# Order within a step of attention: the probabilities' split, transposes and read-back against the dense piece, in a two-layer decoder on one core

## The chip, the cores and the metric

The kernel runs on one core of a Trainium2 chip. A core has a matrix engine (TensorE, PE in the profile; its weight loads are PEld), a vector engine (VectorE, DVE), a scalar engine (ScalarE, ACT), a third elementwise engine (GpSimd, POOL) and SyncE (SP), which only issues DMAs here. Each engine runs its own list of instructions strictly in the order in which it was written; semaphores hold an instruction back until what it reads is there or what it overwrites is free. The metric is the device time of one execution in microseconds (us). Times inside an execution come from one profiled execution and count from its first instruction.

## The reference

A two-layer decoder trunk on 512 tokens of width 1024, batch 1. Layer 1 is chunkwise retention, layer 2 is native sparse attention. The change lies in layer 2. What matters of it, cut:

```python
s_c = q @ k_cmp * scale                      # 31 compressed blocks, masked, softmax -> p_c
imp = selection_importance(p_c.sum(heads))   # top 16 of at most 8 blocks of 64: all are selected
p_s = softmax(where(valid_s, q @ k_sel * scale, NEG))     # causal over 512 keys
p_w = softmax(where(valid_w, q @ k_win * scale, NEG))     # window of 512 keys: causal too
o = g0 * (p_c @ v_cmp) + g1 * (p_s @ v_sel) + g2 * (p_w @ v_win)
y = (silu(gate) * o) @ w_out
```

There are 4 groups of 4 heads; keys and values are shared in a group. With 512 tokens both big branches are plain causal attention with their own keys and values, so each head has two of them. Every product is computed in a split form: each operand is a high part plus a low part, and three matmuls (high-high, high-low, low-high) make one.

## The kernel before, in words

**Passes.** The attention loop has 32 passes, written (g, u): group g = 0..3, u = 0..7. Pass u stands for head u // 2 and branch u % 2 of group g. A pass is software-pipelined: it computes scores and exponentials of the *next* pass (`scores`), scales them (`scale_probs`), splits its *own* transposed probabilities into high and low part (`probs_split`), transposes the next pass's probabilities (`probs_T`), and at its end multiplies its own with the values (`values`). Between these stands dense work, the "fillers": projections of the next group's queries, of the gate, and of the output, cut into units of 12 matmuls. `steps` says how many units go to the three places `fill(0)`, `fill(1)`, `fill(2)` of a pass.

**Names and lines of before.** DVE: L949 and L946 add the causal mask to the scores, L953 takes the row maximum, L962 and L963 make the scale factors, L986 makes the low part `tL`, L975 (four of them) transposes 32x32 blocks of the next probabilities into `pt1`, L205 makes the low part of a weight piece, L757 and L744 finish a gate or query projection, L1021 adds a tile of the output projection to the residual, L900 to L903 finish the compressed branch, L916 splits its transposed probabilities, L999 and L1001 gate the head's output `o`. ACT: L954 takes the exponential and its row sum, L985 makes the high part `tH`, L190 the high part of a weight piece, L756 and L743 begin the evacuation of a projection. POOL: L966 (four) scales the probabilities, L176 multiplies a weight piece by its gain, L904 scales the compressed probabilities. SP: L979 (four DMAs) writes `pt1` to a tile `moved` in DRAM, L982 reads it back permuted into `pt2`, L143 loads a weight piece.

**The transposition.** A full 512-wide transposition is made of 32x32 transposes on DVE, four writes to DRAM and one read-back in another order. The read-back waits for the four writes, and the split (L985, L986) waits for the read-back. SP works in order, so whatever stands behind the read-back waits with it.

**Weights.** `Stream` holds the list of weight pieces. `tick(n)` does n times: low part of the oldest piece (DVE) and the next load (SP), high part of the next (ACT), gain of the next but one (POOL). Four raw buffers and six split buffers stand between.

**Banks.** A projection or an output tile needs a PSUM bank of tag `d`, of which there are two, used in turn; PE may write a bank again only after the DVE instruction that empties it.

**Three kinds of passes** come up below. *Gate-and-tile* passes, (0,4), (1,0), (1,4), (2,0), (2,4), (3,0): two units of a gate projection in `fill(0)` and `fill(1)`, then two output tiles in `fill(2)`. *Tile* passes, (0,5), (1,1), (1,5), (2,1), (2,5), (3,1), (3,5): six output tiles, two in each place. *Projection* passes: (0,0) to (0,3), (1,2), (1,3), (2,2), (2,3) and (3,2), (3,3), with gate and query units only; and the last two passes of a group, (g,6) and (g,7), which also hold the next group's key projections and are followed by its value projections.

Of the kernel before, what the change touches and what calls it, by code (L numbers as in the profile page):

```python
# [11 lines left out]
F32 = mybir.dt.float32  # L12
# [21 lines left out]
def between(g, h):  # L34

    def out(g, pair):
        return [("nout", g, 2 * pair), ("nout", g, 2 * pair + 1)]

    if g == 3:
        return ([("gate", 3, 0)] + out(2, 1), [("gate", 3, 1), ("gate", 3, 2)], out(3, 0),  # L40
                [("gate", 3, 3), ("emb", 1, 0), ("emb", 1, 1)])[h]
    q = [("q", g + 1, h - 1), ("q", g + 1, h)]
    if g == 0 and h < 2:
        return q if h else [("gate", 0, 0), ("gate", 0, 1)]
    return [("gate", g, h)] + (q if h % 2 else out(g - (h == 0), int(h == 0)))
# [191 lines left out]
def decoder(ctx: ExitStack, tc: tile.TileContext, x, xT, stream, cst, msk, gains, fnorm, out):  # L237
    nc = tc.nc
# [3 lines left out]
    dr = ctx.enter_context(tc.tile_pool(name="dr", bufs=2, space=bass.MemoryType.DRAM))  # L242
# [7 lines left out]
    def V(o, n):  # L250
        assert o + n <= nF, (o, n)
        return arenaF[:, o:o + n]
# [20 lines left out]
    def psum(tag, shape=None):  # L273
        n = {"d": 2, "s": 3, "pt": 2, "o": 1}[tag]
        return ps.tile([128, 512], F32, name=tag, bufs=n)
# [26 lines left out]
    W = Stream(nc, stream, raw, wh, wl, gain)  # L302
# [172 lines left out]
    def run(g):  # L475
        for _ in g:
            pass
# [219 lines left out]
    pt1, pt2 = V(fb + 2176, 1280), V(fb + 3456, 1280)  # L697
# [33 lines left out]
    def v_pieces(g):  # L731
        if g == 0:
            return [W.get("kvb", r, min(384, 1024 - r), 0, 304) for r in (0, 384, 768)]
        return [W.get("kvv", 512 * a, 512, 256 * g, 256) for a in (0, 1)]
# [27 lines left out]
    def k_proj(g, b):  # L762
        p = W.get("kv", 0, 1024, 1024 + 512 * b + 128 * g, 128)
        o = psum("d")
        wst(p, o)
        if b == 0:
            m = slice(32 * g, 32 * g + 32)
            pool.tensor_copy(k2H[0][:, :32], kcH[:, m].bitcast(F32))
            pool.tensor_copy(k2L[0][:, :32], kcL[:, m].bitcast(F32))
        e = 0 if b else 32  # L770
        split_psum(k2H[b][:, e:], k2L[b][:, e:], o)
        W.tick()
        p.done()
# [134 lines left out]
    def cmp_T(h):  # L908

        p = psum("pt")  # L910
        for i in range(NT):
            pe.transpose(p[:96, 128 * i:128 * i + 128], pc4[h % 2][:, i].rearrange("p r n -> p (r n)"),
                         ident)
        d = pcat[h % 2]
        act.activation(d[:96], p[:96], AF.Copy)
        dve.tensor_sub(d[64:96], p[64:96], d[64:96].bitcast(F32))  # L916

    def scores(g, u):
        h, b = divmod(u, 2)
        e = 0 if b else 32  # L920
        mx, sm_ = scal(4), scal(4)
        cmp = []

        def block(w, i, lo, hi):
            c = slice(128 * i, 128 * i + 128)
            mm3(w, [(q2H[h][:, c], q2L[h][:, c], k2H[b][:, lo:hi], k2L[b][:, lo:hi])], True, True)

        for bank in ((3,), (2,), (0, 1)):
            o = psum("s")
            f, at = 0, []  # L930
            for i in bank:
                lo = e if i == 3 else 0
                n = 128 * i + 128 + e - lo
                block(o[:, f:f + n], i, lo, lo + n)
                at.append(f + e - lo)
                f += n
            if e and 2 in bank:
                block(o[:, 416:448], 3, 0, 32)
                cmp.append((2, o[:, 0:448].rearrange("p (a n) -> p a n", a=14)[:, 0:14:13]))
            elif e and 0 in bank:  # L940
                cmp.append((0, o[:, 0:480].rearrange("p (a n) -> p a n", a=3)[:, 0:2, :32]))
            if 1 in bank:

                d = bass.AP(tensor=o.tensor, offset=o.offset + e,
                            ap=[list(o.ap[0]), [256 + e, 2], [1, 128]])
                dve.tensor_add(d, d, tri[:, None, :].to_broadcast([128, 2, 128]))  # L946
            else:
                d = o[:, at[0] + 128 * bank[0]:][:, :128]
                dve.tensor_add(d, d, tri)  # L949
            for i, f in zip(bank, at):  # L950
                n = 128 * i + 128
                w = o[:, f:f + n]
                dve.reduce_max(mx[:, i:i + 1], w, axis=mybir.AxisListType.X, negate=True)  # L953
                act.activation(P[:, PO[i]:PO[i] + n], w, AF.Exp, bias=mx[:, i:i + 1],  # L954
                               accum_out=sm_[:, i:i + 1])
        chain = cmp_probs(g, h, cmp) if e else iter(())
        next(chain, 0)
        return sm_, chain

    def scale_probs(g, u, sm_):  # L960
        h, b = divmod(u, 2)
        dve.reciprocal(sm_, sm_)  # L962
        dve.tensor_mul(sm_, sm_, bg[:, :, 12 * g + 3 * h + b + 1])  # L963
        for i in (3, 2, 0, 1):
            w = P[:, PO[i]:PO[i] + 128 * i + 128]
            pool.tensor_scalar(w, w, sm_[:, i:i + 1], 1.0, op0=OP.mult, op1=OP.mult)  # L966

    def view(a, o, *ap):
        return bass.AP(tensor=a.tensor, offset=a.offset + o, ap=[list(a.ap[0])] + [list(d) for d in ap])

    def probs_T():


        for j in range(NT):
            dve.transpose(view(pt1, JB[j], (32, NT - j), (320, 4), (1, 32)),  # L975
                          view(P, PO[j] + 128 * j, (384, NT - j), (32, 4), (1, 32)))
        m = dr.tile([128, 1280], F32, name="moved")
        for a in range(4):
            nc.sync.dma_start(bass.AP(tensor=m.tensor, offset=m.offset + 320 * a,  # L979
                                      ap=[[1280, 32], [32 * 1280, 4], [1, 320]]),  # L980
                              pt1[32 * a:32 * a + 32].rearrange("p (b n) -> p b n", b=4))
        nc.sync.dma_start(pt2, m)  # L982

    def probs_split():
        act.activation(tH, pt2, AF.Copy)  # L985
        dve.tensor_sub(tL, pt2, tH.bitcast(F32))  # L986
# [36 lines left out]
    def fillers(g):  # L1023
        for kind, *i in (b for h in range(4) for b in between(g, h)):
            yield from {"gate": g_proj, "q": q_proj, "nout": pair_tiles, "emb": emb_tiles}[kind](*i)
# [4 lines left out]
    sums, chain = scores(0, 0)  # L1030
    scale_probs(0, 0, sums)
    next(comp1)
    w2p.done()
    probs_T()
    run(chain)
    k_proj(0, 1)

# [3 lines left out]
    for g in range(GROUPS):  # L1041
        f = fillers(g)
        for u in range(8):
            h = u // 2
            last = (g, u) == (3, 7)
            W.auto = False
            left = 2 * len(between(g, h))
            first = 4 if h == 3 else left // 2
            n = PLAN[u] if g == 3 else left - first if u % 2 else first
            steps = [1, 1, 0] if last else PARTS[n]  # L1050

            def fill(i):
                for _ in range(steps[i]):
                    next(f)

            sums = None
            if u < 7:
                nxt = g, u + 1
            elif g < 3:
                k_proj(g + 1, 0)  # L1060
                k_proj(g + 1, 1)
                nxt = g + 1, 0
            else:
                nxt = None
            if nxt:
                sums, chain = scores(*nxt)
            fill(0)
            if sums is not None:
                scale_probs(*nxt, sums)
            next(chain, 0)  # L1070
            fill(1)
            probs_split()
            if sums is not None:
                probs_T()
            W.tick(0 if last else 2)
            next(chain, 0)
            if u % 2 == 0:
                cmp_T(h)
            fill(2)
            if u % 2 == 0:  # L1080
                o_head = psum("o")
            values(g, u, o_head)
            W.auto = True
        run(f)
        if g < 3:
            p = v_pieces(g + 1)
            for t in range(NT):
                v_proj(g + 1, t, p, ("d", "pt")[t % 2], t % 2)
# [101 lines left out]
```

## Time and profile before

| | |
|---|---|
| time, median of 3 runs | 1251.55 us (1251.02 to 1253.88) |
| the profiled execution's own time | 1248.97 us |
| its span, first to last instruction | 1247.2 us |
| PE busy | 1146.7 us, 92% of the span |
| DVE busy | 753.4 us, 60% |
| ACT busy | 485.5 us, 39% |
| POOL busy | 324.9 us, 26% |
| mean granted clock of PE | 0.960 |

The profiled execution is 1.8 us longer than its span and 2.6 us under the median of the runs. Busy shares are means over the whole program: layer 1 and layer 2's projections fill the first 590 us, the attention loop goes from 590 to about 1174 us. In the rows below the first number is a start in us, the second a duration, and square brackets give how long the engine had stood idle before and what ended that.

### The profile page before, as it was taken

To read this page: it belongs to the slowest core of one execution; us is meant where nothing else is said; L and a number is where in the kernel's file an instruction comes from. 1 tells how busy PE (TensorE), PEld (TensorE's weight loads), DVE (VectorE), ACT (ScalarE), POOL (GpSimd) and SP (SyncE) were. 2 spreads that over 40 slices of the span, in tenths; PEclk is the share of its full clock that TensorE was granted. 3 is DMA by queue.
4 is the path that set the end of the run, shared out by engine and by line. 5 is a ranking of instruction groups with operands and counts; after the bars stand their busy time and mean duration, and the time that the engine had idled before them with its cause. 6 is when DMAs were issued, how large, how long until landed. Compare 5 with 4: busy or idle time off the path is not lost. (4 is left out here: it accounts for less than half of the span.)

```text
span 1247.2 us, 14924 instructions
## 1 busy us (share of the span) xinstructions
PE 1146.7 (92%) x5486; PEld 961.9 (77%) x5486; DVE 753.4 (60%) x1290; ACT 485.5 (39%) x852; POOL 324.9 (26%) x357
## 2 busy tenths in 40 slices
PE   9999999999999999997878898879988799878797
PEld 7888888888888888886767787768877688666686
DVE  4745446346435565566666656776576766777455
ACT  6432233233234554464333334442344323443454
POOL 0121012003002123556242304243134422221102
PEclk9999999999999999999788999999999899979899
DMA  8422322322322313454343333443424443353311
GB/s 326 138 73 85 105 85 85 101 93 68 105 81 68 115 39 124 155 161 135 99 150 119 110 118 115 152 135 106 138 83 146 135 135 110 107 170 124 99 51 68
DMA packets 52633, 143.84 MB, mean 115 GB/s; under 512 B 6096, under 2 KB 22736, under 8 KB 52560
## 3 DMA queue, kind: packets, MB, share of 16 engines
q1 hardware_dynamic: 52128, 142.10, 35.4%
q8 instruction: 43, 0.70, 0.2%
q10 hardware_dynamic: 432, 0.79, 0.2%
q14 instruction: 30, 0.25, 0.1%
HBM read 119.80 MB, written 23.07 MB: 115 GB/s over the span
## 5 line engine op out<-in xcount | busy, mean ns | idle before, releaser
L356 PE MATMUL d<-arenaR 128*128 128x512 f32 (+2 forms) x2904 | 686.2, 391 | 39.7 <-DVE arenaF L1021 27.2
L356 PEld LDWEIGHTS d<-arenaR 128*128 128x128 f32 x2904 | 538.4, 193 | 152.9 <-DVE arenaF L1021 32.3
L356 PE MATMUL s<-arenaR 128*128 128x512 f32 (+8 forms) x1182 | 249.1, 363 | 3.4 <-ACT arenaF L954 1.8
L356 PEld LDWEIGHTS s<-arenaR 128*128 128x128 f32 x1182 | 208.6, 197 | 35.1 <-ACT arenaF L954 2.0
L205 DVE TENSOR_TENSOR arenaR<-arenaF,arenaR 128x1024 fp32r<-128x1024 f32 (+1 forms) x142 | 179.6, 1282 | 67.0 <-ACT arenaR L190 66.8
L190 ACT ACTIVATE arenaR<-arenaF 128x1024 fp32r<-128x1024 f32 (+1 forms) x142 | 145.9, 1046 | 120.4 <-PE s L356 68.4
L356 PE MATMUL o<-arenaR 128*128 128x512 f32 (+3 forms) x744 | 148.5, 351 | 42.3 <-ACT arenaR L985 21.9
L356 PEld LDWEIGHTS o<-arenaR 128*128 128x128 f32 x744 | 126.3, 209 | 65.2 <-ACT arenaR L985 25.9
L176 POOL TENSOR_TENSOR arenaF<-arenaF 128x512 f32<-128x512 f32 x108 | 126.2, 1190 | 154.8 <-DMA arenaF<-stream_dram 150.4
L966 POOL TENSOR_SCALAR arenaF<-arenaF 128x512 f32<-128x512 f32 (+3 forms) x128 | 84.5, 678 | 231.2 <-ACT arenaR L985 79.8
L954 ACT ACTIVATE arenaF<-s,arenaF 128x512 f32<-128x512 f32 (+3 forms) x128 | 67.6, 528 | 134.4 <-DVE arenaF L953 132.3
L372 POOL TENSOR_TENSOR arenaF<-arenaF 128x1 f32<-128x1 f32 (+1 forms) x25 | 14.2, 568 | 292.3 <-DVE arenaF L371 292.3
L953 DVE TENSOR_REDUCE arenaF<-s 128x1 f32<-128x512 f32 (+3 forms) x128 | 62.8, 491 | 22.9 <-ACT arenaF L954 19.6
L356 PE MATMUL pt<-arenaR 128*128 128x512 f32 (+1 forms) x384 | 75.9, 349 | 0.0
L975 DVE STREAM_TRANSPOSE arenaF<-arenaF 128x512 f32<-128x512 f32 (+3 forms) x128 | 57.7, 489 | 25.0 <-POOL arenaF L966 23.9
L356 PEld LDWEIGHTS pt<-arenaR 128*128 128x128 f32 x384 | 62.8, 189 | 9.4
L209 DVE SCALAR_TENSOR_TENSOR arenaR<-arenaF,arenaR 128x512 fp32r<-128x512 f32 x64 | 45.7, 762 | 35.0 <-PE pt L356 21.4
L986 DVE TENSOR_TENSOR arenaR<-arenaF,arenaR 128x1280 fp32r<-128x1280 f32 x32 | 50.4, 1575 | 19.6 <-ACT arenaR L985 19.6
L194 ACT ACTIVATE arenaR<-arenaF 128x512 fp32r<-128x512 f32 x64 | 43.1, 720 | 46.5 <-issue 22.3
L1000 ACT ACTIVATE arenaR<-arenaF 128x512 fp32r<-128x512 f32 x16 | 10.1, 633 | 130.0 <-DVE arenaF L999 130.0
L1021 DVE TENSOR_TENSOR arenaF<-arenaF,d 128x512 f32<-128x512 f32 x64 | 42.0, 682 | 25.1 <-PE d L356 24.8
L985 ACT ACTIVATE arenaR<-arenaF 128x1280 fp32r<-128x1280 f32 x32 | 40.6, 1267 | 2.8 <-DMA arenaF<-moved 2.7
(125 smaller groups left out, 741.5 us busy)
## 6 DMA issues: line engine op xcount, KB each, us to landing
arenaF<-stream_dram SPq DMA_DIRECT2D x174, 512.0 KB, 4.2
moved<-arenaF SPq DMA_DIRECT2D x128, 160.0 KB, 2.8
arenaF<-moved SPq DMA_DIRECT2D x32, 640.0 KB, 4.0
arenaF<-xT_dram SPq DMA_DIRECT2D x8, 256.0 KB, 4.8
arenaF<-x_dram SPq DMA_DIRECT2D x4, 512.0 KB, 7.6
out_dram<-arenaF SPq DMA_DIRECT2D x3, 512.0 KB, 2.7
arenaF<-cst_dram SPq DMA_DIRECT2D x4, 256.0 KB, 3.9
arenaF<-stream_dram ACTq DMA_DIRECT2D x2, 256.0 KB, 3.4
```

Of the source, the lines that this page charges most:

```text
L176: self.nc.gpsimd.tensor_mul(r3[:, k], r3[:, k], g[:, k, None].to_broadcast([128, m // 2, w]))
L190: self.nc.scalar.activation(hi[:, :m * w], raw, AF.Copy)
L194: self.nc.scalar.activation(hi[:, c], raw[:, c], AF.Copy, scale=g[:, k:k + 1])
L205: self.nc.vector.tensor_sub(lo[:, :m * w], raw, hi[:, :m * w])
L209: self.nc.vector.scalar_tensor_tensor(lo[:, c], raw[:, c], g[:, k:k + 1], hi[:, c], op0=OP.mult, op1=OP.subtract)
L356: pe.matmul(o, a, b, start=start and i == 0, stop=stop and i == n - 1)
L953: dve.reduce_max(mx[:, i:i + 1], w, axis=mybir.AxisListType.X, negate=True)
L954: act.activation(P[:, PO[i]:PO[i] + n], w, AF.Exp, bias=mx[:, i:i + 1], accum_out=sm_[:, i:i + 1])
L966: pool.tensor_scalar(w, w, sm_[:, i:i + 1], 1.0, op0=OP.mult, op1=OP.mult)
L975: dve.transpose(view(pt1, JB[j], (32, NT - j), (320, 4), (1, 32)), view(P, PO[j] + 128 * j, (384, NT - j), (32, 4), (1, 32)))
L986: dve.tensor_sub(tL, pt2, tH.bitcast(F32))
L1021: dve.tensor_add(d, d, o)
```

## The change

Within a pass the order becomes: scores of the next pass, `fill(0)`, scaling, split of the own probabilities, exponential of the compressed branch, one tick, transposes and writes, `fill(1)`, the second tick, the rest of the compressed branch, `fill(2)`, read-back, values. Before, `fill(1)` stood ahead of the split, both ticks followed the writes and the read-back followed the writes at once. Nothing is computed otherwise. In the new file the lines are shifted: L975 is L977, L979 is L981, L982 is L986, L985 and L986 are L989 and L990, L999, L1001 and L1021 are L1003, L1005 and L1025. The texts keep the old numbers.

```diff
     def probs_T():
         for j in range(NT):
             dve.transpose(view(pt1, JB[j], (32, NT - j), (320, 4), (1, 32)), ...
-        m = dr.tile([128, 1280], F32, name="moved")
+        m = moved[0] = dr.tile([128, 1280], F32, name="moved")
         for a in range(4):
             nc.sync.dma_start(...)
-        nc.sync.dma_start(pt2, m)
+
+    def probs_back():
+        nc.sync.dma_start(pt2, moved.pop(0))
...
             if sums is not None:
                 scale_probs(*nxt, sums)
+            probs_split()
             next(chain, 0)
-            fill(1)
-            probs_split()
+            W.tick(0 if last else 1)
             if sums is not None:
                 probs_T()
-            W.tick(0 if last else 2)
+            fill(1)
+            W.tick(0 if last else 1)
             next(chain, 0)
             if u % 2 == 0:
                 cmp_T(h)
             fill(2)
+            if sums is not None:
+                probs_back()
```

DVE in the gate-and-tile pass (1,0), from the scale factors to the next pass's scores, before:

```order
L962 RECIPROCAL arenaF<-arenaF 128x4
L963 TENSOR_TENSOR arenaF<-arenaF 128x4
L757 SCALAR_TENSOR_TENSOR arenaF<-arenaF,d 128x512
L986 TENSOR_TENSOR arenaR<-arenaF,arenaR 128x1280
L975 STREAM_TRANSPOSE arenaF<-arenaF 128x4x4x32
L975 STREAM_TRANSPOSE arenaF<-arenaF 128x3x4x32
L975 STREAM_TRANSPOSE arenaF<-arenaF 128x2x4x32
L975 STREAM_TRANSPOSE arenaF<-arenaF 128x4x32
L205 TENSOR_TENSOR arenaR<-arenaF,arenaR 128x1024
L916 TENSOR_TENSOR arenaR<-pt,arenaR 32x512
L1021 TENSOR_TENSOR arenaF<-arenaF,d 128x512 x2
```

and the same stretch now (L990 is the low part, L977 the transposes, L1025 the tiles' adds):

```order
L962 RECIPROCAL arenaF<-arenaF 128x4
L963 TENSOR_TENSOR arenaF<-arenaF 128x4
L990 TENSOR_TENSOR arenaR<-arenaF,arenaR 128x1280
L977 STREAM_TRANSPOSE arenaF<-arenaF 128x4x4x32
L977 STREAM_TRANSPOSE arenaF<-arenaF 128x3x4x32
L977 STREAM_TRANSPOSE arenaF<-arenaF 128x2x4x32
L977 STREAM_TRANSPOSE arenaF<-arenaF 128x4x32
L757 SCALAR_TENSOR_TENSOR arenaF<-arenaF,d 128x512
L205 TENSOR_TENSOR arenaR<-arenaF,arenaR 128x1024
L916 TENSOR_TENSOR arenaR<-pt,arenaR 32x512
L1025 TENSOR_TENSOR arenaF<-arenaF,d 128x512 x2
```

The evacuation of the gate's bank, L757, has moved from ahead of the low part to behind the transposes.

DVE in the tile pass (1,1), from the adds of `fill(0)`'s tiles to the last low part of a weight piece, before:

```order
L1021 TENSOR_TENSOR arenaF<-arenaF,d 128x512 x2
L962 RECIPROCAL arenaF<-arenaF 128x4
L963 TENSOR_TENSOR arenaF<-arenaF 128x4
L1021 TENSOR_TENSOR arenaF<-arenaF,d 128x512 x2
L986 TENSOR_TENSOR arenaR<-arenaF,arenaR 128x1280
L975 STREAM_TRANSPOSE arenaF<-arenaF 128x4x4x32
L975 STREAM_TRANSPOSE arenaF<-arenaF 128x3x4x32
L975 STREAM_TRANSPOSE arenaF<-arenaF 128x2x4x32
L975 STREAM_TRANSPOSE arenaF<-arenaF 128x4x32
L205 TENSOR_TENSOR arenaR<-arenaF,arenaR 128x1024 x2
```

and now:

```order
L1025 TENSOR_TENSOR arenaF<-arenaF,d 128x512 x2
L962 RECIPROCAL arenaF<-arenaF 128x4
L963 TENSOR_TENSOR arenaF<-arenaF 128x4
L990 TENSOR_TENSOR arenaR<-arenaF,arenaR 128x1280
L205 TENSOR_TENSOR arenaR<-arenaF,arenaR 128x1024
L977 STREAM_TRANSPOSE arenaF<-arenaF 128x4x4x32
L977 STREAM_TRANSPOSE arenaF<-arenaF 128x3x4x32
L977 STREAM_TRANSPOSE arenaF<-arenaF 128x2x4x32
L977 STREAM_TRANSPOSE arenaF<-arenaF 128x4x32
L1025 TENSOR_TENSOR arenaF<-arenaF,d 128x512 x2
L205 TENSOR_TENSOR arenaR<-arenaF,arenaR 128x1024
```

The adds of `fill(1)`'s two tiles stand behind the low part, one L205 and the transposes, where they stood ahead of all of them.

SP from the writes of pass (1,1) to those of (1,2), before:

```order
L979 DMA moved<-arenaF 32x4x320 x4
L982 DMA arenaF<-moved 128x1280
L143 DMA arenaF<-stream_dram 128x1024 x2
L979 DMA moved<-arenaF 32x4x320 x4
L982 DMA arenaF<-moved 128x1280
```

and now (L981 the writes, L986 the read-back):

```order
L981 DMA moved<-arenaF 32x4x320 x4
L143 DMA arenaF<-stream_dram 128x1024
L986 DMA arenaF<-moved 128x1280
L143 DMA arenaF<-stream_dram 128x1024
L981 DMA moved<-arenaF 32x4x320 x4
```

Of the two weight loads of a pass one now goes out ahead of the writes and one between the writes and the read-back; before, both stood behind the read-back. POOL's list is the same in both kernels, and so is PE's.

## Rows read from the trace of the kernel before

**Rows 1.** Waits of PE over the whole span: us in total, times, longest

```profile
PE d L356 <- DVE arenaF L1021: 27.2, 16, 3.4
PE o L356 <- ACT arenaR L985: 21.9, 11, 3.0
PE o L356 <- DVE arenaR L986: 13.2, 12, 1.6
PE d L356 <- DVE arenaF L757: 11.9, 4, 4.8
```

**Rows 2.** Timeline, first mask add of a pass, on DVE: start, duration

```profile
606.54 0.29 DVE L949 TENSOR_TENSOR s<-s,masks 128x128 f32<-128x128 f32 x1
...
669.06 0.29 DVE L949 TENSOR_TENSOR s<-s,masks 128x128 f32<-128x128 f32 x1
...
703.25 0.29 DVE L949 TENSOR_TENSOR s<-s,masks 128x128 f32<-128x128 f32 x1
...
753.71 0.29 DVE L949 TENSOR_TENSOR s<-s,masks 128x128 f32<-128x128 f32 x1
...
766.70 0.29 DVE L949 TENSOR_TENSOR s<-s,masks 128x128 f32<-128x128 f32 x1
...
787.05 0.29 DVE L949 TENSOR_TENSOR s<-s,masks 128x128 f32<-128x128 f32 x1
...
821.39 0.29 DVE L949 TENSOR_TENSOR s<-s,masks 128x128 f32<-128x128 f32 x1
```

**Rows 3.** Timeline, the gate-and-tile pass (1,0)

```profile
757.60 0.19 ACT L954 ACTIVATION_READ_ACCUMULATOR arenaF<-s,arenaF 128x1 f32 x1
...
758.17 1.27 ACT L985 ACTIVATE arenaR<-arenaF 128x1280 fp32r<-128x1280 f32 x1
758.31 0.69 DVE L757 SCALAR_TENSOR_TENSOR arenaF<-arenaF,d 128x512 f32<-128x512 f32 x1
758.37 3.29 POOL L966 TENSOR_SCALAR arenaF<-arenaF 128x512 f32<-128x512 f32 x4 [2.69 <-ACT arenaF L756]
...
759.48 1.49 DVE L986 TENSOR_TENSOR arenaR<-arenaF,arenaR 128x1280 fp32r<-128x1280 f32 x1 [0.48 <-ACT arenaR L985]
...
761.69 1.84 DVE L975 STREAM_TRANSPOSE arenaF<-arenaF 128x512 f32<-128x512 f32 x4 [0.73 <-POOL arenaF L966]
```

**Rows 4.** Timeline, the tile pass (1,1)

```profile
772.41 7.36 PE L356 MATMUL d<-arenaR 128*128 128x512 f32 x24 [3.19 <-DVE arenaF L1021]
...
773.42 2.06 POOL L966 TENSOR_SCALAR arenaF<-arenaF 128x512 f32<-128x512 f32 x4 [9.76 <-ACT arenaR L985]
...
780.83 2.32 DVE L205 TENSOR_TENSOR arenaR<-arenaF,arenaR 128x1024 fp32r<-128x1024 f32 x2
...
785.06 0.68 DVE L999 SCALAR_TENSOR_TENSOR arenaF<-o,arenaF 128x512 f32<-128x512 f32 x1
```

**Rows 5.** Timeline, PE behind the gate's bank in pass (1,4)

```profile
826.82 2.73 PE L356 MATMUL d<-arenaR 128*128 128x512 f32 x6 [4.78 <-DVE arenaF L757]
...
831.80 2.50 PE L356 MATMUL s<-arenaR 128*128 128x512 f32 x15
```

**Rows 6.** Busy time in a stretch of that: busy PE, PEld, DVE, ACT, POOL; PEclk, DMA, GB/s

```profile
826.80:829.30 2.50, 2.48 (x6) 1.94 (x7) 1.50 (x1) 2.50 (x4) 2.50 (x4) 0.55 0.00 0
```

**Rows 7.** Timeline, read-back of pass (1,0); page section 6, issue to landing, last number

```profile
767.99 0.34 SPq L982 DMA_DIRECT2D arenaF<-moved  x1
...
arenaF<-moved SPq DMA_DIRECT2D x32, 640.0 KB, 4.0
```

**Rows 8.** Timeline, POOL and DVE behind a weight load, passes (1,2) and (1,3)

```profile
790.57 1.04 POOL L176 TENSOR_TENSOR arenaF<-arenaF 128x512 f32<-128x512 f32 x1 [15.10 <-DMA arenaF<-stream_dram]
...
813.89 1.84 DVE L975 STREAM_TRANSPOSE arenaF<-arenaF 128x512 f32<-128x512 f32 x4 [3.99 <-POOL arenaF L966]
```

**Rows 9.** Timeline, the values' matmuls of pass (0,7)

```profile
735.00 0.50 PE L356 MATMUL o<-arenaR 128*128 128x512 f32 x1 [1.62 <-ACT arenaR L985]
...
736.53 1.96 PE L356 MATMUL o<-arenaR 128*128 128x512 f32 x11 [1.03 <-DVE arenaR L986]
```

More of the change, by code (lines that the diff above doesn't have):

```diff
@@ L969, in view @@
         return bass.AP(tensor=a.tensor, offset=a.offset + o, ap=[list(a.ap[0])] + [list(d) for d in ap])
+    moved = {}
     def probs_T():
@@ L1079, in decoder @@
             fill(2)
+            if sums is not None:
+                probs_back()
             if u % 2 == 0:
```

## The prediction

> **What bounds the kernel now.** I read PE's waits first. PE does nearly all the work, so its waits say what else the end depends on. In the attention loop it waits for two things: for the split of the own probabilities ahead of the values, 21.9 us for the high part and 13.2 us for the low part, and for a `d` bank behind L1021 (27.2) or L757 (11.9) [rows 1]. The change goes at the first kind. The second kind says that PE is often ahead of DVE, so I then took DVE's own clock of the loop: the time from one pass's first mask add to the next one's [rows 2]. Pass (1,0) takes 766.70 - 753.71 = 12.99 us and pass (1,1) 20.35; the four passes (0,0) to (0,3) take 62.52, and (1,2) with (1,3) 34.34. DVE works through each pass in order, so a pass lasts as long as DVE's list with its waits, unless PE or the read-back is later. The forecast is made by laying the new list of each kind of pass out with the durations of before, from the first mask add as zero.
>
> **Gate-and-tile passes (six).** Now: L954's last row sum ends 4.08 after the start (757.60 + 0.19) [rows 3]. `tH`, now first behind it on ACT, takes 1.27 and ends at 5.4. The low part takes 1.49, to 6.9. The four L966 on POOL start 4.66 after the start as before and take 3.29 when the low part runs beside them [rows 3], against 2.06 with DVE idle [rows 4]; so they end at 7.95, and the transposes, 1.84, run from 8.0 to 9.8. Only then comes L757, 0.69, to 10.5. Before, it ended at 5.3 (758.31 + 0.69) [rows 3]. The second output tile needs the bank that L757 empties. PE has its first tile done long before, and stands. From there on PE is the path: second tile, values, then the next scores, for which DVE waits. The trace has this very stall once, in pass (1,4), 4.78 us, and from its end to the first score matmul it took 831.80 - 826.82 = 4.98 us [rows 5]. The granted clock in the first 2.5 us of it was 0.55 [rows 6], that is near the 1.2 GHz level, after PE had stood. I take 4.98, and 0.7 us as an estimate for the first three score matmuls and the hand-over: 10.5 + 4.98 + 0.7 = 16.2, where (1,0) had 12.99. That is 3.2 us lost. At the full clock the tile is 2.5 x 0.55 = 1.4 and the values 1.96 [rows 9], 3.36 together, and the pass is 14.6.
>
> **Tile passes (seven).** L966 starts 6.7 after the start (773.42 - 766.70) [rows 4], since `fill(0)`'s adds stand ahead of it. The low part and one L205 (2.32 / 2 = 1.16 [rows 4]) now run beside it, to 9.35. If L966 takes 3.29 it ends at 10.0; if L205, which has two operands in SBUF too, delays it in proportion (1.23 x 1.16 / 1.49 = 0.96, an estimate), at 11.0. Transposes to 11.85 or 12.85, then the first of `fill(1)`'s adds, to 12.55 or 13.55. PE has the two tiles of `fill(1)` done at 8.5 (5.7 + 2 x 1.4) and stands 4 to 5 us for that bank. Then come two tiles, the compressed branch's matmul and the values: at the full clock 2.8 + 0.23 + 1.96 = 5.0, with the clock fallen 4.98 - 3.36 = 1.6 more. So L999 starts at 19.2 or 20.2, and the next pass 1.99 later (785.06 to 787.05) [rows 2, 4]: 21.2 or 22.2, where (1,1) had 20.35. In exchange the stall of 3.19 before `fill(1)`'s first tile [rows 4] shrinks to about 1, because the score matmuls come later.
>
> A gate-and-tile pass and the tile pass behind it make 37.4 or 38.4 together. The six pairs took 34.19 (669.06 to 703.25) for the first, 33.34 for the second [rows 2], and 31.8 to 33.6 for the others, 199.5 in all: 24.9 or 30.9 us lost. The seventh tile pass, (3,5), loses 2.0.
>
> **Projection passes.** Here no tile waits for a bank, and the new order does what the waits ask for. Before, POOL's L176 stood for a load (15.10) that was behind the read-back on SP, the scaling stood behind L176, and DVE's transposes stood 3.99 for the scaling [rows 8]; now the load goes ahead of the writes, and the wait goes. What is late next is the read-back: it goes out 6.3 us after the transposes start (767.99 - 761.69) and lands 4.0 later [rows 3, 7], so the next `tH` can start 10.3 after the transposes. (1,2) then lasts 12.5: low part to 6.9, L205 to 8.05, transposes to 9.9, L757, L205 and L916 to 12.5. In (1,3) `pt2` is there at 8.05 + 10.3 - 12.5 = 5.9, `tH` to 7.2, low part to 8.7, L205 to 9.85, transposes to 11.7, the rest of DVE's list, 4.6, to 16.3. The pair is 28.8, or 30.4 with the longer L966, where it was 34.34: 5.5 or 3.9 gained, twice. The four passes of group 0 come to 56.2 or 57.7 against 62.52: 6.3 or 4.8 gained. (3,2) to (3,4) lose 0.3 or 1.9, since their waits were small.
>
> **Last passes of groups 0 to 2.** These are bound by PE, with 1.62 + 1.03 us before the values [rows 9]. Now the split is ready when PE gets there, but for about 0.1: 2.5 gained each, 7.6 in all. Weight pieces are ready several pieces ahead in both orders; one tick moved costs nothing there.
>
> **Sum.** Lost 26.9, gained 6.3 + 11.1 + 7.6, lost 0.3: +2.2 us. With the longer L966: 32.9 - 4.8 - 7.9 - 7.6 + 1.9 = +14.5. L966 will be delayed by L205 only where both run at once, which is part of the time, so I take the middle, +8.4, against the profiled execution's 1248.97: 1257.4. The median of the runs lay 2.6 above that execution, which makes 1260.
>
> **A rule against the middle.** In rows 3 the low part of 1.49 cost L966 1.23. The Trainium skill, SBUF — State Buffer, section "Who interferes with whom", says that a DVE instruction with two SBUF inputs contends with a GpSimd instruction that reads SBUF, and that the loser blocks entirely. The trace nearly agrees with it (1.23 of 1.49); no run here shows it for L205 against L966. By the row's proportion the sum is the longer one above, by the rule it is that of rival (b).
>
> **Rivals.** (a) *The clock holds and L966 is short.* The bank waits stay, but PE runs on at the full level: the gate-and-tile pass takes 14.6, the tile pass 21.2 - 1.6 = 19.6. The pairs take 34.2 each, 205, so 5.7 lost instead of 24.9, and (3,5) loses 0.4: 5.7 + 0.4 - 25.0 + 0.3 = -18.6, 1233. It decides the sign as soon as more than some five of the thirteen stalls pass without a fall. For it: a fall is not certain after a short stand, the 2.65 us of pass (0,7) were followed by 1.96 for eleven value matmuls [rows 9]. Against it: after 3.19 the 24 matmuls took 7.36, at clock 0.55 after 4.78 [rows 4, 6], and the new stalls are 4 to 5.
> (b) *L966 is shut out for the whole of both low parts* (2.06 + 1.49 + 1.16 = 4.7 in a tile pass): 0.45 more in seven, 0.26 in six, 2 in the projection passes, +21: 1273.
> (c) *The read-back lands late.* The second load now goes out just ahead of it on the same queue, 512 KB beside 640 KB. Where the read-back sets the pass (some six projection passes), 1 to 2 us each would be lost: +16 with the middle sum, 1268. Against it: the loads end soon, about 2 us before the read-back's data would start (an estimate).
> (d) *Gains and losses cancel*, +-2.5: 1251 to 1254, if the truth lies at the short end of the sum.
>
> **How the numbers follow.** Forecast (+5 to +15, 1256 to 1267): 0.42. (a), with a part of its falls: 0.26. (b) 0.10, (c) 0.10, (d) 0.12. This measurement can tell 0.2%, 2.5 us, from no change. Faster is (a), and slower the forecast, (b) and (c): 0.26, 0.12, 0.62. The range for 8 in 10 leaves out the far ends of (a) and (b): 1236 to 1271; the forecast's own is 1256 to 1267.
>
> **What would show it.** In the changed profile: PE's waits for L985 and L986 together under 12 us, those for L757 over 20 us in six or more times, with L1021 still above 20. The gate-and-tile passes should last 15 to 17 us, (1,1) 21 to 22.5, (1,2) with (1,3) 28.5 to 31. POOL's waits for the stream should lie ahead of L904 or vanish, never ahead of L966. L966's four should take 3.3 to 4.3 in tile passes. The forecast is wrong if PE's clock stays at the full level after the bank waits, if the gate's bank is not what the second tile waits for, or if the projection passes end under 27 us a pair.

## The result, and the profile after

The changed kernel takes 1281.88 us (median of 4 runs, 1278.11 to 1283.37) against 1251.92 for the kernel before in the same comparison: ratio 1.0233, 95% interval 1.0207 to 1.0258. It is slower, as forecast, but by 30 us and not by 8, and outside the range. The profiled execution took 1282.42 us, its span is 1280.6, and the mean granted clock fell from 0.960 to 0.947.

PE's waits, which answer to [rows 1] (us in total, times, longest; L1025 is L1021 of before, L989 and L990 are L985 and L986):

```profile
PE d L356 <- DVE arenaF L1025: 43.1, 15, 4.7
PE d L356 <- DVE arenaF L757: 32.4, 8, 7.6
PE o L356 <- ACT arenaR L989: 24.9, 7, 8.1
PE o L356 <- DVE arenaR L990: 11.7, 11, 1.5
```

The two waits for a `d` bank have grown from 39.1 to 75.5 us. The two waits for the split, at which the change goes, are 36.6 where they were 35.1; the forecast wanted them under 12. The passes, by their first mask adds ([rows 2] shows those of before; start, duration):

```profile
757.63 0.29 DVE L949 TENSOR_TENSOR s<-s,masks 128x128 f32<-128x128 f32 x1
...
774.04 0.30 DVE L949 TENSOR_TENSOR s<-s,masks 128x128 f32<-128x128 f32 x1 [2.76 <-PE s L356]
...
797.48 0.29 DVE L949 TENSOR_TENSOR s<-s,masks 128x128 f32<-128x128 f32 x1
...
810.98 0.30 DVE L949 TENSOR_TENSOR s<-s,masks 128x128 f32<-128x128 f32 x1
...
829.69 0.29 DVE L949 TENSOR_TENSOR s<-s,masks 128x128 f32<-128x128 f32 x1
```

So (1,0) went from 12.99 to 16.41 us, (1,1) from 20.35 to 23.44, and (1,2) with (1,3) from 34.34 to 32.21. The second of these five rows says what the pass waited for: DVE stood 2.76 for PE's scores. Summed over all passes by kind (time from a first mask add to the next, us; (3,6) is the last pass with a mask add, and its line runs to the end of the program):

| passes | before | after | difference | forecast, middle |
|---|---|---|---|---|
| six gate-and-tile, seven tile | 218.79 | 261.33 | +42.54 | +29.9 |
| (0,0) to (0,3) | 62.52 | 60.99 | -1.53 | -5.55 |
| (1,2), (1,3), (2,2), (2,3) | 68.66 | 64.44 | -4.22 | -9.4 |
| last passes of groups 0 to 2 | 153.52 | 143.91 | -9.61 | -7.6 |
| (3,2) to (3,4) | 40.30 | 43.50 | +3.20 | +1.1 |
| (3,6) to the end | 96.87 | 100.04 | +3.17 | 0 |
| sum | | | +33.55 | +8.4 |

The span grew by 33.4. The timeline of (1,0), against [rows 3]:

```profile
762.30 3.37 POOL L966 TENSOR_SCALAR arenaF<-arenaF 128x512 f32<-128x512 f32 x4 [1.77 <-DVE arenaF L963]
...
765.70 1.84 DVE L977 STREAM_TRANSPOSE arenaF<-arenaF 128x512 f32<-128x512 f32 x4 [1.29 <-POOL arenaF L966]
767.47 0.65 DVE L757 SCALAR_TENSOR_TENSOR arenaF<-arenaF,d 128x512 f32<-128x512 f32 x1
...
768.17 1.75 PE L356 MATMUL d<-arenaR 128*128 128x512 f32 x6 [3.68 <-DVE arenaF L757]
...
773.15 2.50 PE L356 MATMUL s<-arenaR 128*128 128x512 f32 x15
```

L757 now ends at 768.12, 10.49 us after the pass began, and PE starts the second tile behind it, after standing 3.68. In (1,1), against [rows 4], it is the same with `fill(1)`'s adds:

```profile
780.78 4.21 POOL L966 TENSOR_SCALAR arenaF<-arenaF 128x512 f32<-128x512 f32 x4 [13.11 <-DVE arenaF L963]
...
785.03 1.84 DVE L977 STREAM_TRANSPOSE arenaF<-arenaF 128x512 f32<-128x512 f32 x4 [1.88 <-POOL arenaF L966]
786.79 1.25 DVE L1025 TENSOR_TENSOR arenaF<-arenaF,d 128x512 f32<-128x512 f32 x2
787.50 5.49 PE L356 MATMUL d<-arenaR 128*128 128x512 f32 x12 [4.66 <-DVE arenaF L1025]
...
795.48 0.69 DVE L1003 SCALAR_TENSOR_TENSOR arenaF<-o,arenaF 128x512 f32<-128x512 f32 x1 [1.76 <-PE o L356]
```

Read upwards: the transposes stood 1.88 for the scaling, which took 4.21 beside both low parts; PE stood 4.66 for the first add behind the transposes. Then its matmuls ran slowly. The stretch from 787.5 (busy PE, PEld, DVE, ACT, POOL; PEclk, DMA, GB/s) answers to [rows 6]:

```profile
787.50:793.00 5.50, 5.50 (x13) 4.34 (x14) 3.65 (x7) 0.00 (x0) 2.10 (x3) 0.50 0.85 227
```

0.50 is the 1.2 GHz level. The read-back, against [rows 7], in (1,2) and (1,3):

```profile
806.68 1.84 DVE L977 STREAM_TRANSPOSE arenaF<-arenaF 128x512 f32<-128x512 f32 x4 [1.21 <-POOL arenaF L966]
...
814.23 0.34 SPq L986 DMA_DIRECT2D arenaF<-moved  x1
...
818.57 1.27 ACT L989 ACTIVATE arenaR<-arenaF 128x1280 fp32r<-128x1280 f32 x1 [2.92 <-DMA arenaF<-moved]
```

It goes out 7.55 us after the transposes start, where it was 6.3, and `tH`, which starts 4.34 us after that, has stood 2.92 for it. The page's list of DMA issues (last number: median from issue to landing) has the rest, 5.1 against 4.0 of before:

```profile
arenaF<-moved SPq DMA_DIRECT2D x32, 640.0 KB, 5.1
```

### The profile page after: what moved, and what is told of

Its sections match the earlier page's. It is cut to its first block, busy times and chain, and to the rows that moved or that the text cites. A ratio compares the mean times of both kernels' runs of the same rounds, so it can differ in the third digit from the quotient of the medians.

```text
span 1280.6 us, 14890 instructions
## 1 busy us (share of the span) xinstructions
PE 1148.9 (90%) x5486; PEld 962.4 (75%) x5486; DVE 760.2 (59%) x1290; ACT 483.1 (38%) x852; POOL 359.0 (28%) x357
## 5 line engine op out<-in xcount | busy, mean ns | idle before, releaser
L356 PE MATMUL d<-arenaR 128*128 128x512 f32 (+2 forms) x2904 | 696.6, 395 | 77.3 <-DVE arenaF L1025 43.1
L205 DVE TENSOR_TENSOR arenaR<-arenaF,arenaR 128x1024 fp32r<-128x1024 f32 (+1 forms) x142 | 187.4, 1329 | 66.9 <-ACT arenaR L190 66.8
L966 POOL TENSOR_SCALAR arenaF<-arenaF 128x512 f32<-128x512 f32 (+3 forms) x128 | 108.1, 863 | 308.0 <-DVE arenaF L963 217.4
L356 PE MATMUL o<-arenaR 128*128 128x512 f32 (+3 forms) x744 | 145.5, 346 | 42.1 <-ACT arenaR L989 24.9
L176 POOL TENSOR_TENSOR arenaF<-arenaF 128x512 f32<-128x512 f32 x108 | 136.1, 1282 | 72.8 <-DMA arenaF<-stream_dram 68.4
L372 POOL TENSOR_TENSOR arenaF<-arenaF 128x1 f32<-128x1 f32 (+1 forms) x25 | 14.3, 570 | 293.5 <-DVE arenaF L371 293.5
L977 DVE STREAM_TRANSPOSE arenaF<-arenaF 128x512 f32<-128x512 f32 (+3 forms) x128 | 57.8, 490 | 35.6 <-POOL arenaF L966 34.4
L990 DVE TENSOR_TENSOR arenaR<-arenaF,arenaR 128x1280 fp32r<-128x1280 f32 x32 | 50.6, 1582 | 42.4 <-ACT arenaR L989 42.3
L1004 ACT ACTIVATE arenaR<-arenaF 128x512 fp32r<-128x512 f32 x16 | 10.1, 631 | 156.4 <-DVE arenaF L1003 156.4
L1025 DVE TENSOR_TENSOR arenaF<-arenaF,d 128x512 f32<-128x512 f32 x64 | 41.9, 679 | 20.1 <-PE d L356 19.8
L989 ACT ACTIVATE arenaR<-arenaF 128x1280 fp32r<-128x1280 f32 x32 | 40.5, 1267 | 31.0 <-DMA arenaF<-moved 31.0
```

Of the source, the lines that this page charges most:

```text
L176: self.nc.gpsimd.tensor_mul(r3[:, k], r3[:, k], g[:, k, None].to_broadcast([128, m // 2, w]))
L205: self.nc.vector.tensor_sub(lo[:, :m * w], raw, hi[:, :m * w])
L356: pe.matmul(o, a, b, start=start and i == 0, stop=stop and i == n - 1)
L1025: dve.tensor_add(d, d, o)
```

## The experiments

The theories: **B**, PE waits for a `d` bank whose emptying instruction now stands behind the transposes; **R**, the read-back comes too late; **S**, the early split beside the scaling does the harm; **K**, the granted clock that falls behind the stalls makes much of the loss; the others stand in the expectations. The first four kernels shared their runs of the kernel before (1248.23 us), the next four theirs (1250.17), the last two theirs (1247.87).

**1. The early split alone.** Against the kernel before:

```diff
                 scale_probs(*nxt, sums)
+            probs_split()
             next(chain, 0)
             fill(1)
-            probs_split()
             if sums is not None:
                 probs_T()
```

> Order of the kernel before, with one part of the change alone: the split of the own probabilities stands ahead of fill(1), as in the changed kernel; transposes, writes and read-back follow fill(1) together, both ticks behind them. Theory B (the loss is PE waiting for a d bank whose emptying instruction stands behind the transposes): here only the low part, 1.5 us, stands ahead of that instruction, so the bank waits do not grow, the gains in the last passes stay (some 8 us) and the tile passes shorten by up to 2 us: 1222 to 1240 us, faster than before; PE's waits for L757 under 8 us. Theory S (the early split itself does the harm, since the low part runs beside the scaling on POOL): the passes lengthen as in the changed kernel in part, 1255 to 1275 us. Theory R (the read-back issued at the step's end lands too late) has nothing against this kernel and expects it at or under the time of before, 1235 to 1252.

1233.48 us, ratio to before 0.9875 (0.9833 to 0.9918): faster, as B expects; S falls. The gain lies in the tile passes, 13.6 us; the gate-and-tile passes cost 1.3. One number missed: PE's waits for L757 are not under 8 us but 25.1. They grow when only the low part stands ahead of L757, and yet the passes hardly lengthen: (1,0) takes 13.29 us with a stand of 3.15 us. The last passes gained 1.4 us, not 8: in each (g,7) the stand for the split is gone, but PE now stands 1.4 us for L205, the low part of a weight piece.

**2. The late read-back alone.** Against the kernel before:

```diff
                 probs_T()
...
             fill(2)
+            if sums is not None:
+                probs_back()
```

with `probs_back` taken out of `probs_T` as in the change.

> Order of the kernel before, with another part alone: the read-back is issued at the step's end, behind both weight loads. Theory R (the late read-back makes the loss): the split waits for it in the gate-and-tile and projection passes, 1262 to 1290 us, and ACT's waits for DMA of the read-back at 25 us or more. Theory B: no bank wait is lengthened; 1245 to 1258 us, the stalls of POOL for a weight load falling from 150 us to under 80.

1244.05 us, ratio 0.9947 (0.9919 to 0.9974), a little faster, 1 us under B's range. R is no cause of the loss by itself: the four passes (1,2) to (2,3) gain 6.7 us, (3,2) to (3,4) lose 1.0 and the end 2.4. Waits of POOL's L176 for a load fell only to 125.0 from 150.4 us, not under 80, and those of ACT for the read-back were 19.3.

**3. The read-back ahead of the second tick.** Against the changed kernel:

```diff
             fill(1)
+            if sums is not None:
+                probs_back()
             W.tick(0 if last else 1)
...
             fill(2)
-            if sums is not None:
-                probs_back()
```

> The changed kernel, with the read-back issued ahead of the second tick, so that on SP it follows the writes at once and the second weight load stands behind it. Theory R: the changed kernel's loss comes back by 15 us or more, 1255 to 1267 us. Theory B: only the projection passes gain, some 1.5 us in each of eight, and no gate-and-tile or tile pass by over 0.5 us: 1268 to 1280 us. Waits of ACT for the read-back fall from 31 us to under 10 by both.

1273.72 us, ratio 1.0194 (1.0140 to 1.0248). That interval overlaps the changed kernel's, so the times do not tell them apart; the spans, 1272.8 and 1280.6, differ by 7.8. The read-back lands in 3.9 us, ACT's waits for it fall from 31.0 only to 19.2. It is a small part, as B expects; experiment 10 settles its size.

**4. The old place of fill(1) in the thirteen passes.** Against the changed kernel, where `tiles` holds for the gate-and-tile and tile passes and (3,4):

```diff
+            if tiles:
+                next(chain, 0)
+                fill(1)
             probs_split()
-            next(chain, 0)
+            if not tiles:
+                next(chain, 0)
             W.tick(0 if last else 1)
             if sums is not None:
                 probs_T()
-            fill(1)
+            if not tiles:
+                fill(1)
```

> The changed kernel, but in the thirteen gate-and-tile and tile passes and in (3,4) fill(1) stands ahead of the split, and with that ahead of the transposes, as in the kernel before; first tick ahead of the transposes, second behind them, read-back at the end stay. Theory B: the thirteen passes come back to the periods of before, some 40 us off the changed kernel: 1237 to 1252 us. Theory R: the read-back is late in them as elsewhere, 1262 us or more. Theory S: the part of the loss that the low part beside the scaling makes comes back, some 10 to 15 us: 1266 to 1272.

1239.04 us, ratio 0.9927 (0.9901 to 0.9954). The thirteen passes come to 221.24 us, 40 off the changed kernel's 261.33, and the last passes of groups 0 to 2 gain another 5.9. R and S expected 1262 or more: both fall as main causes.

**5. Spare banks, the order untouched.** PSUM has a tag `pt` with two banks, used for the compressed branch's transposes. In the changed kernel, the second output tile of `fill(2)` in gate-and-tile passes and both in tile passes take a `pt` bank:

```diff
     def pair_tile(c, t, p):
-        o = psum("d")
+        o = psum("pt" if spare.get(t % 2) else "d")
...
```

(cut: the lines in the loop that set `spare` ahead of `fill(2)` in these passes and clear it behind).

> The changed kernel, its order untouched on DVE, ACT, POOL and SP; only PE's banks differ: the output tiles of fill(2) that waited for a d bank go into the two banks of tag pt, which are free there (the second tile in the gate-and-tile passes, both in the tile passes). Theory B: the stall ahead of fill(2)'s tiles goes, and with it the fall of the clock; gate-and-tile passes come to some 14, tile passes to 19 to 20 us, that is 13 x 3 to 3.5 us off: 1235 to 1248 us. Theory S (the early split beside the scaling) and theory R (the read-back) leave the time as it is, 1275 us or more.

1237.33 us, ratio 0.9907 (0.9882 to 0.9933). This is B's sharpest test: the lists of DVE, ACT, POOL and SP are the changed kernel's, and 44.5 us are gone against its median. In the traces the thirteen passes are 39.8 us shorter than in the changed kernel and the last passes of groups 0 to 2 are 7.1 shorter. The gate-and-tile passes take 14.4 us in the mean, the tile passes 19.3. Its waits of PE (L1027 is L1025):

```profile
PE o L356 <- ACT arenaR L989: 29.1, 9, 6.6
PE d L356 <- DVE arenaF L1027: 26.4, 8, 4.5
PE o L356 <- DVE arenaR L990: 16.5, 15, 1.8
...
PE d L356 <- DVE arenaF L757: 1.4, 2, 1.1
```

The waits for L757 went from 32.4 to 1.4. Its pass (1,1):

```profile
770.24 4.60 PE L356 MATMUL d<-arenaR 128*128 128x512 f32 x12 [3.65 <-DVE arenaF L1027]
771.24 4.43 POOL L966 TENSOR_SCALAR arenaF<-arenaF 128x512 f32<-128x512 f32 x4 [10.26 <-DVE arenaF L963]
...
774.68 2.89 PE L356 MATMUL pt<-arenaR 128*128 128x512 f32 x12
775.70 1.84 DVE L977 STREAM_TRANSPOSE arenaF<-arenaF 128x512 f32<-128x512 f32 x4 [1.21 <-POOL arenaF L966]
```

The scaling is no shorter than before the edit, 4.43 against 4.21, and the transposes wait for it. It costs the pass little: PE is at `fill(2)`'s tiles, in `pt`, before the transposes have begun.

**6. Extra matmuls in the stand.** Against the changed kernel, 28 matmuls of 256 columns into a `pt` bank, ahead of `fill(2)` in the tile passes and between its two tiles in the gate-and-tile passes; nothing reads them.

```diff
+    def keep(n):
+        w = psum("pt")
+        for _ in range(n):
+            pe.matmul(w[:, :256], masks[:, :128], masks[:, :256], start=True, stop=True)
...
```

(cut: the calls `keep(28)` at the two places).

> The changed kernel, and PE does 28 extra matmuls of 256 columns (some 3 us at the full clock) into a free bank where it would stand waiting for the d bank in the thirteen passes: their results are not read. Theory K (half of the loss is the granted clock that falls after the stall): the tile and the values behind it run at the full level and 1.6 to 2.5 us come back in each pass, 1250 to 1262 us, mean clock 0.960 or more. Theory W (the wait alone counts, or the extra matmuls do not hold the clock): within 5 us of the changed kernel, 1277 to 1287 us.

1264.35 us, ratio 1.0125 (1.0102 to 1.0148), mean clock 0.972. By the medians 17.5 us come back, just short of K's range. The tile passes are 144.78 us where they were 159.83, 2.15 each. Its (1,1):

```profile
776.00 3.23 PE L1026 MATMUL pt<-masks 128*128 128x256 bf16 x28
...
780.85 3.04 PE L356 MATMUL d<-arenaR 128*128 128x512 f32 x12 [1.62 <-DVE arenaF L1034]
...
786.09 0.69 DVE L1003 SCALAR_TENSOR_TENSOR arenaF<-o,arenaF 128x512 f32<-128x512 f32 x1 [0.68 <-PE o L356]
```

```profile
780.85:786.35 5.50, 5.50 (x27) 4.72 (x28) 4.72 (x9) 0.00 (x0) 2.30 (x3) 1.00 0.81 215
```

From the freed bank to L1003 it is 5.24 us here (780.85 to 786.09), at clock 1.00, and 7.98 in the changed kernel (787.50 to 795.48), at 0.50 in its first 5.5 us. The bank comes no earlier: the adds start 12.75 us into the pass in both (780.15 - 767.40, and 786.79 - 774.04). So 2.7 us of that pass are the clock alone. The gate-and-tile passes gained 4.1 us in all. Where the stand is longer than the extra work the clock falls all the same, as in (1,4), and that pass is longer than in the changed kernel (18.55 against 16.86). A part of this is not the clock: the bank comes 11.54 us after the start there, 1.0 later than in the changed kernel.

```profile
823.20 3.23 PE L1026 MATMUL pt<-masks 128*128 128x256 bf16 x28
...
831.83 2.93 PE L356 MATMUL d<-arenaR 128*128 128x512 f32 x6 [5.39 <-DVE arenaF L757]
```

**7. Both ticks behind fill(1).** Against the changed kernel:

```diff
             next(chain, 0)
-            W.tick(0 if last else 1)
             if sums is not None:
                 probs_T()
             fill(1)
-            W.tick(0 if last else 1)
+            W.tick(0 if last else 2)
```

> The changed kernel with the first tick moved behind fill(1), beside the second: no low part of a weight piece (L205) stands ahead of the transposes any more, so in the tile passes the scaling on POOL has only the low part tL beside it. Theory B with the scaling's length as a term of its own: L966's four fall from 4.2 to 3.3 us in the tile passes and their transposes start 1 us earlier; 7 x 1 us, and up to 1 us in each of eight projection passes: 1268 to 1277 us. Theory P (L205 is only shoved elsewhere, and the scaling's length decides nothing, since PE waits for DVE's whole list): 1279 to 1285 us.

1277.09 us, ratio 1.0217 (1.0188 to 1.0246): at the edge of B's range, and not to be told from the changed kernel. The trace shows why. In tile passes the scaling is shorter, and they gain 7.9 us; in each (g,7) the tick is now late for its weight piece (L205), PE stands 1.98 or 1.99 us for it, and the last passes give back 10.1:

```profile
780.26 3.16 POOL L966 TENSOR_SCALAR arenaF<-arenaF 128x512 f32<-128x512 f32 x4 [12.88 <-DVE arenaF L963]
...
902.89 1.90 PE L356 MATMUL d<-arenaR 128*128 128x256 f32 x11 [1.99 <-DVE arenaR L205]
```

**8. The order by kind of pass.** Gate-and-tile passes and (3,4) as in the kernel before; tile passes with the split ahead of `fill(1)`, and transposes, read-back and ticks behind it; all others as in experiment 3.

```diff
+            if kind == "gate":
+                next(chain, 0)
+                fill(1)
+                probs_split()
+            else:
+                probs_split()
+                next(chain, 0)
+            if kind == "tile":
+                fill(1)
+            if kind is None:
+                W.tick(0 if last else 1)
...
```

> An order by kind of pass: the gate-and-tile passes and (3,4) as in the kernel before; the tile passes with the split ahead of fill(1), and transposes, read-back and ticks behind it; the projection and last passes as in the changed kernel, with the read-back ahead of the second tick. If the gains of the single runs add up (tile passes -13.6, last passes -10 to -15, projection passes -6, group 0 -1.6 against the kernel before): 1211 to 1222 us. If they exclude one another, since a gain in one pass is given back in the next: 1228 to 1240 us.

1223.86 us, ratio 0.9799 (0.9783 to 0.9816): 2.0% under the kernel before, and faster than both kernels. It lies outside both expected ranges, 2 us above the first: the gains add up but for a few us. Against the kernel before, the tile passes keep 8.0 of 13.6, the last passes gain 14.3, and the gate-and-tile passes lose 3.0.

**9. That order with the spare banks.** Experiments 8 and 5 together (the edit is the one line of 5).

> The order by kind of pass, and with it the two spare banks for the output tiles of fill(2). Theory B: that order still has PE waiting for a d bank behind L1025 and L757, 24.9 + 4.9 us in its trace, of which fill(2)'s share goes: tile passes 0.5 to 1 us shorter each, gate-and-tile passes 0 to 0.5: 1214 to 1221 us. If PE is the path in them by its own work and not by those waits: 1222 to 1226 us.

1225.14 us, ratio 0.9816 (0.9779 to 0.9853), no gain over 8, inside the second range. The waits for L757 went from 4.9 to 0.7 us, those for the tiles' adds from 24.9 to 26.2: what was left there was not on the path.

**10. The changed order with both corrections.** Experiments 5 and 3 together (both edits as shown).

> The changed kernel's order on DVE, ACT and POOL with both corrections: the spare banks for fill(2)'s tiles, and the read-back ahead of the second tick. If the two causes are separate and add up, the -44.5 us of the banks and the -8.2 of the read-back against the changed kernel make 1225 to 1233 us. If the read-back's part was the same time counted twice (a late read-back hidden behind a bank wait or the reverse): 1235 to 1240 us.

1225.34 us, ratio 0.9817 (0.9787 to 0.9846), against 0.9907 (0.9882 to 0.9933) with the banks alone: 0.9%, some 11 us, and the intervals do not overlap. The spans differ by 9.7. So the read-back's place behind the second load is a cause of its own, and the two add up, inside the first range. PE's waits for L989, 29.1 in experiment 5, are 20.1 in it, and the read-back's landing went back from 5.2 to:

```profile
arenaF<-moved SPq DMA_DIRECT2D x32, 640.0 KB, 3.9
```

## Why the prediction was right in sign and wrong in size

**What bounds the kernel.** Right. PE's stand for a `d` bank behind the transposes is the loss: of the 42.5 us that the thirteen passes grew by, moving `fill(2)`'s tiles to other banks takes away 39.8 (experiment 5), and moving `fill(1)` back 40.1 (experiment 4). Three steps of the sum failed, and they are named below: the price of the fallen clock in the tile passes, the late read-back that was set at nothing, and the middle for the length of L966.

**Gate-and-tile passes**, forecast 16.2 us, measured 16.9 in the mean (101.50 / 6). The working came out by its steps: PE gets the bank 10.53 to 10.61 us after the start in five of the six (forecast 10.5). From there to the next pass it is 5.8 to 6.7 us in five (forecast 4.98 + 0.7 = 5.7), and 4.3 in (3,0), where the clock held; (3,0) took 14.86, and the forecast had 14.6 for that. The exception is (0,4) with 19.36: its bank comes only after 13.54 us, since `tH` stood for the read-back there and one L205 ran ahead of the transposes. POOL's L176 ran beside the low part, which took 2.37 us there and not 1.49, and beside a part of that L205 (2.06 us):

```profile
672.91 1.28 ACT L989 ACTIVATE arenaR<-arenaF 128x1280 fp32r<-128x1280 f32 x1 [1.33 <-DMA arenaF<-moved]
...
674.21 3.29 POOL L176 TENSOR_TENSOR arenaF<-arenaF 128x512 f32<-128x512 f32 x2
674.23 2.37 DVE L990 TENSOR_TENSOR arenaR<-arenaF,arenaR 128x1280 fp32r<-128x1280 f32 x1 [2.23 <-ACT arenaR L989]
676.52 2.06 DVE L205 TENSOR_TENSOR arenaR<-arenaF,arenaR 128x1024 fp32r<-128x1024 f32 x1
678.50 1.64 DVE L977 STREAM_TRANSPOSE arenaF<-arenaF 128x512 f32<-128x512 f32 x3
...
680.96 2.93 PE L356 MATMUL d<-arenaR 128*128 128x512 f32 x6 [5.84 <-DVE arenaF L757]
```

The late read-back and the bank wait, two cases in the text, act in one chain here. A small reading was off too: the values' 1.96 in [rows 9] is for eleven of their twelve matmuls, and (3,0) has 2.09 for all.

**Tile passes**, forecast 21.2 or 22.2, measured 22.83 in the mean. Two steps failed, the choice of the middle and the price of the clock. L966 took 4.21 in (1,1), the long end (forecast 3.29 or about 4.3): low part and L205 run beside it in six of the seven tile passes, so the middle was half a us short in each. In the seventh, (3,5), no L205 does, and it took 21.41. The fallen clock was priced at 1.6 us, from the tile and the values of (1,4), that is one tile; here two tiles run behind the stand, and experiment 6 shows 2.7. From the freed bank to L1003 it was 7.98 and not 6.65; up to the freed bank the long layout was right within 0.1 us.

**The rule on the shared port.** The Trainium skill, SBUF — State Buffer, section "Who interferes with whom", has the loser blocked entirely. The four L966 take 2.07 with nothing beside them ((0,4) of the changed kernel), 3.16 in experiment 7 with the low part beside, and 4.21 in the changed kernel with the low part and L205. So 1.49 + 1.2 us of DVE's work cost 2.1. By the rule it would have been 4.7; the trace lies nearer to the proportion that the forecast took for its long end.

**Projection passes**, forecast gains 5.55 and 9.4, measured 1.53 and 4.22. The failing step is the late read-back, which the sum put at nothing and rival (c) set aside because the loads end soon. The read-back was issued 7.55 us after the transposes, not 6.3, and landed in 5.1 (median), not 4.0; and the transposes of (1,2) stood for the longer scaling, 9.2 after the start where 8.05 was worked out. In (1,3) `tH` started 7.6 after the start and not 5.9. Experiment 10 gives this its price, some 10 us against experiment 5: 4.8 of them in the eight projection passes, 3.9 in the thirteen, 1.3 in (3,2) to (3,4) and 1.4 from (3,6) to the end, less 1.3 lost in the last passes. The end is a place that the sum did not have: it is 3.2 longer than before in the changed kernel, 2.4 in experiment 2, and 0.6 with the read-back ahead of the second tick (experiment 10).

**Last passes**, forecast 7.6 gained, measured 9.6. The number is near, and that is luck: it is the three (g,7) with 15.7 gained and the three (g,6) with 6.1 lost. In (g,7) the stand for the split is gone, as forecast. But the premise that weight pieces are ready several pieces ahead failed: with the early split and both ticks late, PE stands for L205 in its place, and the last passes gain 1.4 (experiment 1) or lose 0.4 (experiment 7). The first tick, which the sum gave nothing, is worth 10.1 us there by its place ahead of `fill(1)` (experiment 7 against the changed kernel). The 6.1 belong to the bank wait: experiments 4 and 5 give 6.2 and 6.6 us of it back. PE comes into (1,6) with 27 matmuls of the fillers to do before and 36 in the changed kernel:

```profile
854.56 6.29 PE L356 MATMUL d<-arenaR 128*128 128x512 f32 x27
...
869.33 8.36 PE L356 MATMUL d<-arenaR 128*128 128x512 f32 x36
```

PE's waits for L989 and L990 in the whole program stayed, since the projection passes of group 0 and group 3 and the pass (3,7) now stand for the read-back, once 8.09.

**The sum.** Of 25 us missed, 12.6 are in the thirteen passes, two thirds of it in the tile passes, 9.3 in gains that did not come, 3.2 at the end. In (1,1), which took 1.7 us more than the middle, 1.1 is the clock (2.7 us where the sum had 1.6) and half a us the middle. The rivals (b) and (c) were given 0.10 each, as alternatives to the forecast; of (b) the long scaling came, though not its 4.7 us, and (c) came in part, both together with the forecast. A price that adds to the others had been treated as a case that excludes them. Rival (a) falls: behind five of the six stands for L757 in the gate-and-tile passes the clock fell, and held only in (3,0), whose tile and values took 1.67 and 2.09 us:

```profile
1088.57 1.67 PE L356 MATMUL d<-arenaR 128*128 128x512 f32 x6 [3.44 <-DVE arenaF L757]
1090.08 2.09 PE L356 MATMUL o<-arenaR 128*128 128x512 f32 x12
```

**What stays open.** The price of the longer scaling by itself: experiment 7 shortened it and gained 7.9 us in the tile passes, but gave 10.1 back in the last passes, so the two can't be parted by it. With the spare banks the scaling is as long and the tile passes are short, so its price hangs on the bank wait behind it.

## What to carry to other kernels

Where PE has nothing to do until a PSUM bank is free, the instruction that empties it should stand ahead of any stage of its engine that can wait on another engine; if it can't, let the matmuls behind it go to another bank, which paid 44.5 us here. When a step is moved, work out first which bank, buffer or queue is freed behind it, and price the stall with the clock that follows it, over all the matmuls that then come. Effects that sit in different passes add up, here but for a few us; they aren't rivals of one another. A wait that goes may uncover the next one, as the wait for the split uncovered that for L205.

## What the runs showed of the hardware

The clock behind a stand of PE doesn't follow from the stand's length alone: after 3.56 us, in (2,0), the next six matmuls took 2.93; after 3.68, in (1,0), they took 1.75 and the values behind them 3.59, so that the fall came late; after 3.44, in (3,0), there was none. Extra matmuls without any use, 3.2 us in each of thirteen stands, made the kernel some 17 us faster (experiment 6). The DVE low part of 1.49 us took 2.37 with POOL's L176 beside it in (0,4) of the changed kernel. A read-back of 640 KB with a load of 512 KB just ahead of it on its queue lands in 5.0 to 5.3 us (medians of the changed kernel and experiments 2, 4, 5, 6 and 7), with the load behind it in 3.9 or 4.0 (the kernel before and experiments 1, 3, 8, 9 and 10).

```profile
928.12 2.93 PE L356 MATMUL d<-arenaR 128*128 128x512 f32 x6 [3.56 <-DVE arenaF L757]
...
769.72 3.59 PE L356 MATMUL o<-arenaR 128*128 128x512 f32 x12
```
